# Four array quarters for the scan's products of two head pairs, and a normalised input made by scaling and plain transposes

## The chip, the cores and the metric

The kernel runs on one core of one Trainium2 chip. The metric is the device time of one execution in microseconds (us). Single durations are given in us or ns.

## What is computed

A two-layer block for 1024 latent tokens and a context of 256 tokens, width 1024. Each layer normalises and modulates its input, projects it with one large matrix, feeds four groups with the columns, multiplies each group's output by its own gate path, and projects back. Group A is a gated DeltaNet with 4 heads of width 64, scanned forward and backward over chunks of 64 tokens; the context runs first and hands its states to the latent tokens.

```python
def rmsnorm(x, g):
    return x * rsqrt(mean(x * x, -1) + EPS) * g
...
h = rmsnorm(x, norm_g[l]) * (1.0 + scale) + shift        # latent; the same for the context
p = h @ w_in[l]
...
# one chunk of the scan, per head; tinv, attn, w, u come from the chunk's own keys and gates
def step(s, xs):
    qg_i, kdec_i, u_i, w_i, attn_i, gl_i = xs
    v_new = u_i - w_i @ s
    o_i = qg_i @ s + attn_i @ v_new
    s = s * gl_i + einsum('bhcd,bhce->bhde', kdec_i, v_new)
    return s, o_i
```

## The kernel before

**How the program is ordered.** Every operation is recorded with the tiles it reads and writes (`Program.record`, `add`). Then `schedule` deals the operations to five engines (PE, ACT, DVE, POOL, SP) by estimated costs (`estimate`), by a priority that is the place in the program less a boost (the scans' is 800), and by when pool buffers come free. The result is a fixed order on each engine. All DMAs go out from SP's queue, in its order. All operations are recorded by one helper, so every row of the trace shows line L214; the names of tiles tell the work apart (`sc`, `ax`, `mm` are PSUM tiles; `mm` is the projections').

**The streams.** Threads write the program: for each layer a context stream and a latent stream. `dense` runs the projections one after the other (products of 128x512, `mm<-hh,w`, `mm<-hl,w`); they are what PE does between the instructions of scans, inversions and normalisations.

**The normalised input.** A tile x of 128 tokens by 1024 gets its factor r per token from `h_stat`. `h_diag` writes the diagonal matrix diag(r) on DVE (`dg`); `h_cols` takes it as the moving operand of four fp32 products per half tile, x(128x128)ᵀ·diag(r), which scale and transpose at once, and splits the modulated result in two parts for the projections. There are 20 tiles: 2 of the context and 8 latent ones at the start, and 10 at the layer boundary (`hstage`, whose tiles 0 to 7 also store the new x to DRAM first).

**Heads and halves.** 64 rows of the array hold one half p of the partitions. `st.qk[hh]`, with hh the pair of heads (0 and 1, or 2 and 3), has head 2·hh + p on half p. The state S is [128, 2 (direction d), 2 (hh), 64], with the same halves.

**Before the scan.** `pair_matrices` forms the chunk matrices and stores them to DRAM: three DMAs `zd<-b` per call, 20 calls. `invert` reads them back as single rows, inverts blocks of 32, and `prep` in `scan` puts together the inverse `Ts` and the matrices `ATs` for four chunks at a time. `gdn` makes decays (`ex`), norms (`norms`) and gates.

**The scan.** One step handles chunk s forward and chunk n−1−s backward. For each of the 8 combinations of d, hh and p there is one product of each kind, 64x64 by 64x64 in fp32, two instructions each:

- kS (bank A, part 0), then x = kS · gate + nk on DVE
- out of the step before (AT · v1), then `out_add`
- T·x (bank A, part 1), then v2 on DVE and v1 on ACT
- qS (bank Bk, part 0), then at = qS · gate on DVE
- Sp = kstᵀ · v2, then S = gs + Sp on DVE

All of them read rows of half p and write columns of half p, as in

```python
self.mm(A[half[p], 0, d, hh, :], st.qk[hh][half[p], 1, tok(d)], S[half[p], d, hh, :])
```

PSUM banks: `psx` rotates through four scan banks and `ax`; a scan holds banks 0 to 3 for A, Sp and two Bk.

## Time and profile before

| | |
|---|---|
| median of 3 runs | 1384.72 us (1384.66 to 1385.25) |
| profiled execution | 1382.8 us |
| its span | 1381.1 us |
| mean granted TensorE clock | 0.969 of 2.4 GHz |
| PE / DVE / ACT busy | 1299.9 / 986.2 / 539.9 us |

How to read it: the profiled execution is one run with its own time; the span is what the trace covers of it, 1.7 us less. The busy time of PE counts products; weight loads (PEld) run beside them. Matmuls are pipelined and overlap, so a group's mean duration is more than its distance from one start to the next; prices per instruction are therefore read from starts in a timeline. The first 165 us hold the modulation vectors, the first normalisations and the first projections; layer 0 goes on to about 680 us; at the boundary (to about 797 us) layer 0's output projection makes the new x; then comes layer 1, with its pair matrices and context scan before and its latent scan from about 1108 to 1206 us, and the output projection in the last 80 us.

### The profile page before, as it was taken

How to read it: one execution, taken by the hardware profiler on the slowest of the kernel's cores; microseconds unless marked ns; L12 is line 12 of the kernel's file. 1: busy time of each engine (PE TensorE's matmuls, PEld its weight loads, DVE VectorE, ACT ScalarE, POOL GpSimd, SP SyncE). 2: the span in 40 equal slices, each digit the busy share in tenths (PEclk: the TensorE clock that was granted, in tenths of full speed). 3: DMA queues.
4: the chain of work that ended last, by engine and by line, in shares of the span. 5: the costliest groups of instructions: out<-in, count | busy, mean ns of one | idle time of the engine just before them, and what ended most of it. 6: DMA issues, size and time to landing. Idle time of an engine off the chain costs nothing.

```text
span 1381.1 us, 27009 instructions
## 1 busy us (share of the span) xinstructions
PE 1299.9 (94%) x10992; PEld 1047.1 (76%) x10992; DVE 986.2 (71%) x2102; ACT 539.9 (39%) x903; POOL 11.9 (1%) x76
## 2 busy tenths in 40 slices
PE   6887899999999999999999999998999888999997
PEld 4886778987778666678887788987777776788886
DVE  3888959999869755753466659899788866753554
ACT  4877433254644221321244355343475121231221
POOL 1000000000000000000000000000000000000000
PEclk9988899999999999999999999999899989999999
DMA  9748232322485566561333341523237533122831
GB/s 306 213 109 242 58 74 70 86 47 61 111 203 145 151 198 190 185 184 54 109 115 111 100 113 51 128 54 88 66 99 178 121 80 100 49 76 96 269 82 56
DMA packets 308465, 166.74 MB, mean 121 GB/s; under 512 B 148254, under 2 KB 292982, under 8 KB 308342
## 3 DMA queue, kind: packets, MB, share of 16 engines
q1 hardware_dynamic: 308342, 165.03, 43.3%
q8 instruction: 86, 1.41, 0.4%
q14 instruction: 37, 0.30, 0.1%
HBM read 124.32 MB, written 35.42 MB: 116 GB/s over the span
## 4 chain that ended last, share of the span: by engine, by line
PE 60%; DVE 15%; DMA 14%; ACT 3%; issue 3%; SPq 3%; ACTq 0%; DVEq 0%
PE mm L214 45%; PE sc L214 11%; DVE u L214 8%; DMA x<-u 6%; PE ax L214 5%; DVE b L214 3%; SPq L214 3%; DMA r<-in_w_in 3%; DVE w L214 2%; DMA u<-in_w_out 2%; ACT u L214 1%; DMA whh<-in_w_ada 1%; DMA whl<-in_w_ada 1%; DMA u<-in_x 1%; DMA b<-zb 1%
## 5 line engine op out<-in xcount | busy, mean ns | idle before, releaser
L214 PE MATMUL mm<-hh,w 128*128 128x512 f32 x1664 | 541.4, 401 | 1.7 <-ACT w L214 1.2
L214 PEld LDWEIGHTS mm<-hh,w 128*128 128x128 f32 x1664 | 311.8, 190 | 82.0 <-issue 16.5
L214 PE MATMUL mm<-hl,w 128*128 128x512 f32 x832 | 334.3, 402 | 0.0
L214 PE MATMUL mm<-u,w 128*128 128x512 f32 (+1 forms) x1320 | 261.5, 356 | 1.6 <-ACT g L214 1.1
L214 PEld LDWEIGHTS mm<-u,w 128*128 128x128 f32 x1320 | 220.0, 193 | 35.3 <-ACT g L214 1.7
L214 DVE SCALAR_TENSOR_TENSOR u<-u,pv,u 128x1024 f32<-128x1024 f32 (+1 forms) x172 | 201.9, 1182 | 1.0
L214 PEld LDWEIGHTS mm<-hl,w 128*128 128x128 f32 x832 | 157.9, 190 | 40.7 <-issue 9.3
L214 ACT CAST w<-r 128x1024 fp32r<-128x1024 f32 x88 | 92.5, 1051 | 214.4 <-PE mm L214 159.2
L214 ACT ACT_TABLE_LOAD x94 | 120.6, 1283 | 17.7 <-DMA zd<-b 5.9
L214 DVE TENSOR_TENSOR w<-r,w 128x1024 fp32r<-128x1024 f32 x88 | 107.2, 1218 | 27.3 <-ACT w L214 26.8
L214 DVE TENSOR_TENSOR u<-u,b 128x256 f32<-128x256 f32 (+25 forms) x246 | 89.3, 378 | 26.5 <-DMA u<-in_x 16.3
L214 PE MATMUL mm<-u,u 128*128 128x256 f32 (+1 forms) x384 | 56.5, 299 | 9.8 <-ACT u L214 4.2
L214 DVE TENSOR_TENSOR b<-u 128x108 f32<-128x108 f32 (+21 forms) x180 | 56.5, 323 | 7.0 <-DMA u<-zd 3.8
L214 PEld LDWEIGHTS mm<-u,u 128*128 128x128 f32 x384 | 51.2, 200 | 12.8 <-DVE u L214 5.0
L214 ACT ACTIVATE b<-u 128x512 f32<-128x512 f32 (+1 forms) x71 | 42.5, 609 | 40.4 <-DVE u L214 29.4
L214 PEld LDWEIGHTS sc<-v,u 64*64 64x64 f32 x1184 | 40.3, 138 | 16.0 <-DVE v L214 9.9
L214 PEld LDWEIGHTS sc<-s,u 64*64 64x64 f32 x1168 | 40.6, 141 | 15.1 <-DVE s L214 4.5
L214 PE MATMUL sc<-s,u 64*64 64x64 f32 x1168 | 47.3, 230 | 2.3 <-DVE u L214 1.7
L214 PE MATMUL sc<-v,u 64*64 64x64 f32 x1184 | 46.6, 226 | 2.5 <-DVE v L214 1.3
L214 PE MATMUL mm<-u,hh 128*128 128x272 f32 x256 | 48.5, 289 | 0.0
L214 ACT ACTIVATE b<-sc,mod,modG 128x128 f32<-128x128 f32 x76 | 30.9, 459 | 44.5 <-PE sc L214 26.9
L214 PE MATMUL sc<-dg,u 128*128 128x128 f32 x248 | 38.2, 311 | 8.7 <-issue 4.7
(271 smaller groups left out, 1451.8 us busy)
## 6 DMA issues: line engine op xcount, KB each, us to landing
r<-in_w_in SPq DMA_DIRECT2D x90, 512.0 KB
u<-in_w_ada SPq DMA_DIRECT2D x16, 1024.0 KB
u<-in_x SPq DMA_DIRECT2D x16, 512.0 KB
r<-ylat SPq DMA_DIRECT2D x16, 512.0 KB
zd<-b SPq DMA_DIRECT2D x60, 128.0 KB
ylat<-g SPq DMA_DIRECT2D x24, 256.0 KB
u<-in_w_out SPq DMA_DIRECT2D x12, 512.0 KB
at<-b SPq DMA_DIRECT2D x36, 128.0 KB
```

The costliest lines, as they stand in the source:

```text
L214: op.alts[e] = ((lambda fn=fn, ar=ar, k=k: fn(*ar, **k)), cost, table)
```

## The change

**Quarters.** For heads 2 and 3 (hh = 1) one side of q, k, the state's partner tensors and the chunk matrices is kept on the other half: the row half of a product is p, its column half p ^ hh. `S`, `v2` and `kst` stay as they were, so kS and qS go from half p to half p ^ hh, T·x goes back, out goes over again, and Sp stays on its half. For that, the gates (`gd`), `nkv` (`shuffle`), the `zd` stores and the rows of `w_out` are written flipped for hh = 1, and the decays and norms get small products that carry a half across (`Rm` split in columns, `pf`): seven more per stream, four streams. Each hh has its own PSUM bank (`scan_pair`, [128, 2, 512]).

**Order in a step.** qS and out are written right behind kS, in one pair of banks Bk with Sp; at comes ahead of the step's gs and v2.

**Stores.** Each of the three `zd` stores of a call becomes three: 60 become 180.

**Input.** `h_turn` scales half a tile by r (`affine`, on ACT or DVE as the planner deals it) and turns it with four plain transposes. `h_diag` goes.

**Planner.** A transpose is estimated at 0.12 us, was 0.218; the least for small products is 0.116, was 0.15; quads are divided by 4; dependences in PSUM go by bank, were by tile.

```diff
+    def scan_pair(self, k):
+        return self.nc.own(self.sc.tile([P, 2, 512], F32, tag=f"sc{k}", name=self.nm("sc")), f"sc{k}", 1)
...
-    def h_diag(self, r):
-        dg = self.small("dg", [P, P])
-        self.nc.vector.tensor_scalar(dg, self.ident, r, None, ALU.mult)
-        return dg
+    def h_turn(self, x, r, half):
+        xr = self.blk([P, 4, P])
+        self.affine(xr, x[:, half * 512:(half + 1) * 512].rearrange("p (k c) -> p k c", c=P), r)
+        ps = self.psx([P, 4, P])
+        for k in range(4):
+            self.tr(ps[:, k, :], xr[:, k, :], self.ident)
+        self.free("b")
+        return ps
...
-            ps = self.psx([P, 4, P])
-            for k in range(4):
-                kk = half * 4 + k
-                self.mm(ps[:, k, :], x[:, kk * P:(kk + 1) * P], dg)
+            ps = self.h_turn(x, r, half)
...
-            nc.sync.dma_start(zd[d, 2 * s0:2 * s0 + 4].rearrange("c p i -> p c i"), t)
+            to = zd[d, 2 * s0:2 * s0 + 4].rearrange("(c h) p i -> h p c i", h=2)
+            t = t.rearrange("p (c h) i -> p h c i", h=2)
+            nc.sync.dma_start(to[0], t[:, 0])
+            for p in range(2):
+                nc.sync.dma_start(to[1, (1 - p) * TC:(2 - p) * TC], t[p * TC:(p + 1) * TC, 1])
...
-            A = self.scan_bank(0, [P, 2, 2, 2, HD])
+            A = pair(0, 2)
+            Bk = pair(1, 3) if need_o or not last else None
+            into = lambda bank, r, kind: quads((bank[half[p ^ hh], r, d, hh, :], st.qk[hh][half[p], kind, tok(d)],
+                                                S[half[p], d, hh, :]) for d, hh, p in each)
...
-                for d, hh, p in each:
-                    self.mm(A[half[p], 0, d, hh, :], st.qk[hh][half[p], 1, tok(d)], S[half[p], d, hh, :])
+                into(A, 0, 1)
...
+            if need_o and not first:
+                into(Bk, 0, 0)
             if pend:
-                out(*pend)
-                out_add(*pend)
+                out(Bk, *pend)
+                out_add(Bk, *pend)
+            at = None
+            if need_o and not first:
+                at = self.small("at", sh)
+                nc.vector.tensor_tensor(at, Bk[:, 0], sg(1), ALU.mult)
...
-            for d, hh, p in each:
-                self.mm(A[half[p], 1, d, hh, :], Ts[j % 2][half[p], d, 2 * (G - 1 - i if d else i) + hh, :], x[half[p], d, hh, :])
+            quads((A[half[p], 1, d, hh, :], Ts[j % 2][half[p ^ hh], d, 2 * (G - 1 - i if d else i) + hh, :],
+                   x[half[p ^ hh], d, hh, :]) for d, hh, p in each)
...
-                if not first:
-                    for d, hh, p in each:
-                        self.mm(Bk[half[p], 0, d, hh, :], st.qk[hh][half[p], 0, tok(d)], S[half[p], d, hh, :])
```

What the planner makes of it is seen on three queues.

PE in layer 1's latent scan, one step; `x` is x, `v_` of before's `sc_1592` is v1 for out, `s_94` the state, `u_` the chunk matrices, keys and queries; before:

```order
L214 MATMUL sc_1585<-s_94,u_1237 64x64 x2
L214 MATMUL mm_1509<-hl_978,w_1469 128x512
L214 MATMUL mm_1509<-hh_977,w_1469 128x512 x2
L214 MATMUL sc_1581<-x_1582,u_1414 64x64 x8
L214 MATMUL mm_1509<-hl_978,w_1469 128x512
L214 MATMUL mm_1509<-hh_977,w_1469 128x512 x2
L214 MATMUL sc_1592<-v_1487_1586,u_1239 64x64 x8
L214 MATMUL sc_1585<-v_1488_1587,u_1414 64x64 x8
L214 MATMUL mm_1509<-hl_978,w_1469 128x512
L214 MATMUL sc_1593<-s_94,u_1236 64x64 x2
```

and with the change:

```order
L215 MATMUL sc_1525<-s_94,u_1201 64x64 x2
L215 MATMUL sc_1525<-v_1423_1522,u_1370 64x64 x8
L215 MATMUL mm_1478<-hh_940,w_1450 128x512
L215 MATMUL mm_1478<-hl_941,w_1450 128x512
L215 MATMUL mm_1478<-hh_940,w_1450 128x512 x2
L215 MATMUL mm_1478<-hl_941,w_1450 128x512
L215 MATMUL mm_1478<-hh_940,w_1450 128x512
L215 MATMUL sc_1524<-x_1526,u_1370 64x64 x8
L215 MATMUL mm_1478<-hh_940,w_1450 128x512
L215 MATMUL mm_1478<-hl_941,w_1450 128x512
L215 MATMUL mm_1478<-hh_940,w_1450 128x512 x2
L215 MATMUL sc_1525<-v_1431_1530,u_1203 64x64 x8
```

qS and out moved from behind T·x to kS, and more projection products stand between the groups: from the first to the last T·x of this scan the order before has 71 of them (narrower ones counted by their width), and with the change 136.

PE at the layer boundary, where a tile's normalised input is turned (`u_956` is x, `b_1015` the scaled half); before:

```order
L214 MATMUL mm_1050<-u_934,w_1025 128x512
L214 MATMUL sc_1052<-dg_1051,u_956 128x128 x4
L214 MATMUL mm_1050<-u_934,w_1025 128x512 x2
L214 MATMUL mm_1050<-u_936,w_1025 128x512
L214 MATMUL sc_1054<-dg_1051,u_956 128x128 x4
L214 MATMUL mm_1050<-u_936,w_1025 128x512 x2
```

and with the change:

```order
L215 MATMUL mm_1014<-u_896,w_989 128x512
L215 MATMUL sc_1016<-ident_100,b_1015 128x128 x4
L215 MATMUL mm_1014<-u_896,w_989 128x512 x2
L215 MATMUL mm_1014<-u_899,w_989 128x512
L215 MATMUL sc_1016<-ident_100,b_1018 128x128 x4
L215 MATMUL mm_1014<-u_899,w_989 128x512 x2
```

The turns stand in the same places; the operand is the scaled half in place of x and the diagonal.

SP while the pair matrices of layer 0's latent stream are stored (`at` are the matrices for out, `u_562` the inversion's rows); before:

```order
L214 DMA zd_563<-b_585 128x4x64 x2
L214 DMA at_561<-b_586 128x256 x2
L214 DMA zd_563<-b_590 128x4x64
L214 DMA u_562<-zd_563 32x32x32
L214 DMA u_632<-u_505 32x16x32 x3
L214 DMA u_644<-at_561 128x512
L214 DMA zd_593<-b_594 128x4x64 x2
```

and with the change:

```order
L215 DMA zd_550<-b_556 128x2x64
L215 DMA zd_550<-b_556 64x2x64
L215 DMA at_548<-b_557 128x256 x2
L215 DMA zd_550<-b_556 64x2x64
L215 DMA zd_550<-b_556 128x2x64
L215 DMA zd_550<-b_556 64x2x64 x2
L215 DMA u_624<-at_548 128x512
L215 DMA zd_550<-b_560 128x2x64
L215 DMA zd_550<-b_560 64x2x64 x2
```

Three stores stand where one stood, and the inversion's first read (`u_549<-zd_550` there) has moved some 40 entries further down, behind stores of the second group of chunks (`zd_576`).

## Rows read from the trace of the kernel before

**Rows 1.** Page: engines' busy us, share, instructions; then the chain by engine.

```profile
PE 1299.9 (94%) x10992; PEld 1047.1 (76%) x10992; DVE 986.2 (71%) x2102; ACT 539.9 (39%) x903; POOL 11.9 (1%) x76
PE 60%; DVE 15%; DMA 14%; ACT 3%; issue 3%; SPq 3%; ACTq 0%; DVEq 0%
```

**Rows 2.** Stages: us, busy PE, PEld, DVE, ACT, POOL (instructions), PEclk, DMA share, GB/s.

```profile
0.00:165.00 165.00, 130.52 (x1007) 115.93 (x1008) 125.88 (x388) 108.44 (x212) 5.31 (x46) 0.91 0.66 191
165.00:680.00 515.00, 505.07 (x4682) 385.95 (x4681) 363.47 (x687) 175.33 (x261) 2.67 (x12) 0.99 0.46 125
...
797.00:1050.00 253.00, 248.22 (x1773) 203.73 (x1772) 219.92 (x389) 123.03 (x178) 2.42 (x8) 0.97 0.37 90
...
1108.00:1206.00 98.00, 88.59 (x1756) 69.25 (x1757) 65.17 (x153) 23.48 (x50) 0.00 (x0) 0.93 0.28 75
```

**Rows 3.** Timeline of PE, 540 to 560 us: start, us, form, instructions.

```profile
541.77 1.15 PE L214 MATMUL sc<-s,u 64*64 64x64 f32 x32
542.85 1.58 PE L214 MATMUL ax<-u,u 128*64 128x128 f32 x16
...
548.79 0.75 PE L214 MATMUL ax<-b,b 32*32 32x32 f32 x64
549.47 0.50 PE L214 MATMUL mm<-hl,w 128*128 128x512 f32 x1
...
558.26 0.68 PE L214 MATMUL sc<-x,u 64*64 64x64 f32 x16
558.87 0.59 PE L214 MATMUL ax<-b,sel 128*2 128x256 f32 x2
```

**Rows 4.** One-column run (timeline), and stages inside a run on shared rows.

```profile
422.40 2.75 PE L214 MATMUL sc<-ones,b 64*64 64x1 f32 x88
...
274.24:274.50 0.26, 0.25 (x4) 0.26 (x5) 0.00 (x0) 1.00 0.00 0
274.50:274.68 0.18, 0.18 (x10) 0.18 (x9) 0.00 (x0) 1.00 0.00 0
```

**Rows 5.** Timelines of PE where tiles are turned: boundary, start, and transposes.

```profile
802.46 3.73 PE L214 MATMUL sc<-dg,u 128*128 128x128 f32 x32
805.94 0.48 PE L214 MATMUL mm<-hl,w 128*128 128x512 f32 x1
...
128.80 3.47 PE L214 MATMUL sc<-dg,u 128*128 128x128 f32 x16 [2.27 <-issue]
...
584.38 1.70 PE L214 MATMUL sc<-ident,u 128*128 128x128 f32 x12
586.01 0.59 PE L214 MATMUL ax<-b,sel 128*2 128x256 f32 x2
```

**Rows 6.** Groups by form: operation, busy us, mean ns of one, idle before.

```profile
L214 DVE TENSOR_SCALAR aux<-aux,rs 128x512 f32<-128x512 f32 x1 | 0.5, 486 | 0.0
L214 ACT ACTIVATE aux<-aux,rs 128x512 f32<-128x512 f32 x1 | 0.7, 722 | 1.0 <-DVE rs L214 1.0
L214 DVE TENSOR_SCALAR dg<-ident,rs 128x128 f32<-128x128 f32 x20 | 5.6, 281 | 0.4
```

**Rows 7.** Chain of 690 to 830 us, and a timeline row of PE there.

```profile
by line: DMA x<-u 59.0%; PE mm L214 16.9%; DMA r<-in_w_in 5.4%; DVE w L214 3.5%; issue 3.1%; DMA u<-in_ctx 2.6%; DVE u L214 2.0%; PE sc L214 1.9%; SPq L214 1.8%; ACT u L214 1.6%; ACT w L214 0.7%; DVE b L214 0.5%; DVE rt L214 0.4%; DVE ss L2
689.90 7.25 PE mm L214 x32
708.09 13.46 DMA x<-u
...
749.85 1.16 PE L214 MATMUL ax<-dg,u 128*128 128x128 f32 x8 [1.16 <-DVE dg L214]
```

**Rows 8.** SP's stores to zd (ns least/median/most), and chain of 380 to 475 us.

```profile
L214 SPq DMA_DIRECT2D zd<-b x60: 360/470/1896, 92.5 to 1069.6; - x60
by line: SPq L214 18.4%; PE sc L214 15.4%; PE mm L214 13.3%; DVE u L214 11.6%; DVE b L214 10.0%; DMA zb<-u 5.6%; DMA at<-b 5.4%; issue 4.5%; PE ax L214 3.5%; DMA gd<-g 2.8%; DMA b<-zb 2.7%; ACT L214 1.4%; DVE w L214 1.2%; DMA b<-in_b_ada 1.
```

**Rows 9.** DVE's operation of the form of at, least/median/most ns.

```profile
L214 DVE TENSOR_TENSOR x<-sc,sg x38: 405/424/426, 196.0 to 1202.2; 128x256 f32<-128x256 f32 x38
```

More of the change, by code (lines that the diff above doesn't have):

```diff
@@ L223, in add @@
                         continue
[L224 removed]
+                    reg = self.region(a)
                 else:
@@ L477, in __init__ @@
         self.n = self.xi = self.scanning = 0
+        self.other = None
         self.W = Weave()
@@ L517, in psx @@
     def psx(self, shape):
-        self.xi = (self.xi + 1) % 5
-        if self.scanning or self.xi == 4:
-            return self.nc.own(self.ax.tile(shape, F32, tag="ax", name=self.nm("ax")), "ax", 1)
-        return self.scan_bank(self.xi, shape)
-    def scan_bank(self, k, shape):
-        return self.nc.own(self.sc.tile(shape, F32, tag=f"sc{k}", name=self.nm("sc")), f"sc{k}", 1)
+        if self.scanning:
+            self.other = None
+        t, self.other = self.other, None
+        if t is None:
+            self.xi = (self.xi + 1) % 3
+            if self.scanning or self.xi == 2:
+                return self.nc.own(self.ax.tile(shape, F32, tag="ax", name=self.nm("ax")), "ax", 1)
+            pair = self.scan_pair(self.xi)
+            t, self.other = pair[:, 0], pair[:, 1]
+        n = 1
+        for x in shape[1:]:
+            n *= x
+        t = t[0:shape[0], 0:n]
+        if len(shape) == 3:
+            t = t.rearrange("p (a b) -> p a b", b=shape[2])
+        elif len(shape) == 4:
+            t = t.rearrange("p (a b c) -> p a b c", b=shape[2], c=shape[3])
+        return t
+    def scan_pair(self, k):
+        return self.nc.own(self.sc.tile([P, 2, 512], F32, tag=f"sc{k}", name=self.nm("sc")), f"sc{k}", 1)
     def mm(self, out, lhsT, rhs, start=True, stop=True):
@@ L1343, in gdn @@
         pe = self.psx([P, 6, m])
+        half = [slice(p * TC, (p + 1) * TC) for p in range(2)]
         for d in range(2):
-            self.mm(pe[:, d], self.Rm[d], g[:, d])
+            self.mm(pairs(pe)[:, d, :, 0], self.Rm[d], pairs(g)[:, d, :, 0])
+            for p in range(2):
+                self.mm(pairs(pe)[half[p], d, :, 1], self.Rm[d][:, half[1 - p]], pairs(g)[:, d, :, 1])
             self.mm(pe[:, 2 + d], self.Lm[d], g[:, d])
@@ L1366, in gdn @@
         st.nk = V("nk", 1)[:, 0]
-        nc.vector.tensor_tensor(st.nk, nq[:, 1], rn[:, 1], ALU.mult)
+        nc.vector.tensor_tensor(t[:, 1], nq[:, 1], rn[:, 1], ALU.mult)
+        pf = self.psx([P, 1, m])
+        self.mm(pairs(pf)[:, 0, :, 0], self.ident, pairs(t)[:, 1, :, 0])
+        for p in range(2):
+            self.mm(pairs(pf)[half[p], 0, :, 1], self.ident[:, half[1 - p]], pairs(t)[:, 1, :, 1])
+        nc.vector.tensor_copy(st.nk, pf[:, 0])
         wd = S("wd", [P, 2, 32])[:, :, :m]
@@ L1419, in norms @@
         nc, n = self.nc, st.n
-        pq = self.psx([P, 2 * n])
-        for b0, nb in st.blocks:
-            for hh in range(2):
+        for hh in range(2):
+            pq = self.psx([P, n])
+            for b0, nb in st.blocks:
                 yield self.room("b")
@@ L1584, in scan, with quads, out, out_add @@
         pend = None
-        def out(s, i, bank, v1, at):
-            AT = ATs[s // G % 2]
-            for d in range(2):
-                for hh in range(2):
-                    e = 2 * (G - 1 - i if d else i) + hh
-                    for p in range(2):
-                        self.mm(bank[half[p], 1, d, hh, :], AT[half[p], d, e], v1[half[p], d, hh, :])
-        def out_add(s, i, bank, v1, at):
+        pair = lambda k, r: self.scan_pair(k)[:, :, 0:r * P].rearrange("p h (r d e) -> p r d h e", r=r, d=2)
+        def quads(calls):
+            nc.quads = True
+            for c in calls:
+                self.mm(*c)
+            nc.quads = False
+        def out(bank, s, i, v1, at):
+            AT = ATs[s // G % 2]
+            quads((bank[half[p ^ hh], 1, d, hh, :], AT[half[p], d, 2 * (G - 1 - i if d else i) + hh], v1[half[p], d, hh, :])
+                  for d, hh, p in each)
+        def out_add(bank, s, i, v1, at):
             oc = st.o[:, two_of(s, n - 1 - s)].rearrange("p d (h e) -> p d h e", h=2)
@@ L1603, in out_add @@
                 self.two(oc, oc, ot, ALU.add)
+        each = [(d, hh, p) for d in range(2) for hh in range(2) for p in range(2)]
         yield from prep(0)
@@ L1650, in scan @@
                 nc.scalar.copy(v1, A[:, 1])
-                if not first:
-                    at = self.small("at", sh)
-                    nc.vector.tensor_tensor(at, Bk[:, 0], sg(1), ALU.mult)
-                pend = (s, i, Bk, v1, at)
+                pend = (s, i, v1, at)
             yield STEP[1]
@@ L1672, in scan @@
         if need_o:
-            out(*pend)
-            out_add(*pend)
+            Bk = pair(1, 3)
+            out(Bk, *pend)
+            out_add(Bk, *pend)
         self.scanning -= 1
```

56 lines of the change are left out of this document (26 added, 30 removed).

## The prediction

> **What bounds the kernel now.** I read the engine line of the page first, then a table of busy time by stage, then the chain of waits, and last the timelines of the instructions that the change touches. The engine line gives TensorE (PE) 94% of the span, VectorE (DVE) 71%, ScalarE (ACT) 39%; the chain of work that ended last lies on PE for 60% and on DVE and DMA for 15% and 14% [rows 1]. The stages tell these apart [rows 2]. From 165 to 680 us (layer 0: pair matrices, both scans, most projections) PE is busy 505 of 515 us, from 797 to 1050 us (layer 1 up to its latent scan) 248 of 253: there a microsecond taken off PE is a microsecond off the kernel, as long as other products stand ready. In layer 1's latent scan (1108 to 1206 us) it is less full, 88.6 of 98 us, so 9.4 us are waits. In the first 165 us no engine is full (PE 131, DVE 126, ACT 108), and from 680 to 797 us the chain lies on a row of stores: 59% of its time is the store of x, 13.5 us for one, one after the other [rows 7].
>
> **The scan's products.** Four kinds of product per step (kS, qS, T·x, out) now use all four 64x64 quarters of the array, where before only the two on the diagonal worked. By the loop, the context scan of layer 0 has 112 of them (T·x and out in 4 steps of 8, kS and qS in 3), that of layer 1 has 56 (no outputs), and each latent scan 16 x 4 x 8 = 512: together 1192. An fp32 product is two instructions, so 2384. Their present price: a run of 32 starts at 541.77 and the next work at 542.85 us, 1.08 us; a run of 16 takes 558.26 to 558.87, 0.61 [rows 3]. The difference, 0.47 us for 16 more, is 29.4 ns each, with two quarters running side by side, so that one quarter spends 58.8 ns on each. Four at once would be 14.7 ns. The unknown is whether two row halves can feed the same 64 columns at once; no row shows that. Bounds: 14.7 ns if they can; 29.4 if they can't, since two would still pair; above that only if the new sequence also broke the old pairing, for which I see no cause, because neighbours in it still differ in rows and in columns. Two rows speak for the low end. The 32x32 products, four at once, go 64 from 548.79 to 549.47, 0.68 us, 10.6 ns each, so neither issue nor weight loads stop at 14.7 [rows 3]. And where 128-row products of the two column halves share their rows, 10 start in 0.18 us inside a run whose first 4 took 0.26 [rows 4]: sharing rows doesn't keep them apart there. A run with one moving column still takes 2.75 us for 88 = 31 ns [rows 4], so the price is that of a quarter's whole turn, weights and all, and another quarter hides it as well as a second one does now. I take 14.7: 2384 x 14.7 ns = **−35.0 us**, of which 30.1 in the latent scans.
>
> Here the Trainium skill speaks against the change. "TensorE: Matmul & The Clock Gate", Part 3, The mechanism, says that weight loads overlap running products only where the row groups differ; by that, heads 2 and 3 would queue behind heads 0 and 1 on the same rows and the sum would lack its 35 us. The shared rows of [rows 4] disagree with it. "TensorEngine Tiling (Array Packing)", Gotcha 1, says that row tiles can't use one PSUM bank at once; the change gives each head its own bank, and no run of before shows the matter.
>
> Is the freed time used? The new order puts 65 more projection products of 128x512 inside layer 1's latent scan. At 0.227 us each (32 in 7.25 [rows 7]) that is 14.8 us of later work drawn forward, about the 15.1 that this scan frees. The filler exists, so I count the whole.
>
> **Small products added.** Seven more per stream for the crosswise decays and norms, 28 in all, 56 instructions. No row shows their form: as the one-column run they cost 31 ns [rows 4], 1.7 us together; as the full-array diagonal product 0.109 us (below), 6.1 us. They lie between in size, so the middle: **+3.9 us**.
>
> **The normalised input.** Twenty tiles, each in two halves, lose 20 diagonal matrices on DVE (0.281 us each) and 160 fp32 products (320 instructions); they get 40 scalings of 128x512 (ACT 0.722 or DVE 0.486 us, [rows 6]) and 160 transposes. Warm, 32 instructions of the old form take 802.46 to 805.94 = 3.48 us, 0.109 each, 0.87 us per half; at the start of the kernel 16 take 3.47, 0.217 each. Transposes of fp32 128x128 take 584.38 to 586.01 for 12, 0.136 each, 0.54 per half [rows 5]. By place:
> Tiles 0 to 7 of layer 1 (680 to 797 us): each waits for SP's sequence of loads and stores, the store alone 13.5 us a tile, PE too (1.16 us before one run [rows 7]). The change leaves that sequence as it is, and a shorter turn only makes PE wait longer: **0**. If the cover went, 16 halves x 0.33 = 5.3 us would come off.
> Tiles 8 and 9: 4 halves x (0.87 − 0.54) on a full PE: **−1.3 us**.
> First 165 us, 10 tiles: PE loses 160 instructions, 17.4 us warm or 34.7 cold, middle 26, and gets 80 transposes, 10.9; at PE's 79% there, the gain ends at 15.1 x 0.79 = 11.9. If instead DVE and ACT set the pace, 20 scalings at the mean of 0.6 us less 10 diagonals are +9.3. No engine is full, so the middle: **−1.3 us**.
>
> **Stores of the pair matrices.** Each call now issues 9 instead of 3 DMAs to zd, 60 become 180. SP issues one in 0.470 us [rows 8], so 120 are 56.4 us of SP; 48 of them, 22.6 us, go in front of each latent scan. Queued behind them on SP are the at stores, the inversion's reads of zd, and weight loads. Between 380 and 475 us SP's queue is 18.4% of the chain [rows 8], over the whole span 3% [rows 1]. By these shares 56.4 us would cost 10.4 or 1.7. A later scan mostly swaps places with projections, of which both layers have many left behind the scan, so I stay near the low end: **+3 us**, bounds 0 and 22.6 per layer.
>
> **The order in a step.** DVE now takes at (qS times a gate) ahead of v2; the same form costs 0.424 us [rows 9]. Over the 33 steps that have both (15 in each latent scan, 3 in layer 0's context scan) that is 14.0 us added to a chain on DVE that leads to T·x's successor and to S. Projections cover it where they stand ready; in layer 1's scan 9.4 of 98 us were uncovered, 10%, so **+1.4 us**, bounds 0 and 14.0. The move of qS forward costs PE nothing: the same products, grouped.
>
> **Sum.** −35.0 + 3.9 − 1.3 − 1.3 + 3 + 1.4 = −29.3 us. The profiled execution took 1382.8 us, which becomes 1353.5; the median of the runs shown is 1.9 higher, 1384.7, so **1355.4 us**. With each term but the first at its better end: −35 + 1.7 − 1.3 − 11.9 = −46.5, 1338.2. With small products, first stage, stores and step order at 6.1, +9.3, +10.4 and +1.4 the time is 1375.6.
>
> **Rivals.**
> 1. The chain of a step becomes the bound. The scan frees PE time, but a step still goes kS, x, T·x, v2, S with DVE between each, and what DVE gets in addition comes before v2. The 9.4 us of waits in layer 1's scan speak for it, the full PE of layer 0 and the 65 products drawn forward against. If half of the latent scans' 30.1 us is waited away: 1355.4 + 15 = 1370.4.
> 2. The quarters don't run together: products that share a column half wait for each other. For it: no row of before has two row halves on one column half. Against: the 32x32 rows and the shared rows. Then the 35 us are missing: 1355.4 + 35 = 1390.4, slower than before by 6. It decides the sign once a product costs over about 27 ns per instruction, since the other terms sum to +5.7.
> 3. The store queue. If layer 0's and layer 1's scans both start 22.6 us later and the projections behind them don't fill PE meanwhile, 45.2 takes the place of the 3: 1355.4 + 42.2 = 1397.6, slower. It changes sign once more than 32 us of the slip go uncovered. For it: 18.4% of the chain between 380 and 475 us; in the new order the inversion's first read of layer 0's latent zd stands behind the second group's stores. Against: the same stretch has PE full, and the projections behind.
> 4. A least distance between two starts of 64x64 products, somewhere between the 14.7 ns that four quarters would need and today's 29.4. For it: the run with one moving column keeps 31 ns although it moves almost nothing [rows 4]. Against: the 32x32 run at 10.6 ns [rows 3]. Halfway, at 22 ns, 2384 x 7.3 = 17.4 of the 35 us are missing: 1372.8. "TensorE: Matmul & The Clock Gate", Part 1, of the Trainium skill gives such a floor, about 25 ns however narrow the product; by it 24.5 us would be missing, 1379.9. The 32x32 run disagrees with it.
>
> **Chances.** Forecast (quarters at 14.7 ns, 1338 to 1366) 0.62; rival 1 with its milder and harder kinds (1366 to 1380) 0.22; rival 2 0.08; rival 3 0.05; rival 4 0.03. About 0.2%, 2.8 us, is what a measurement of this kernel can tell from no change. Forecast, rival 1 and rival 4 are faster by more: 0.87. Rival 2 with a better first stage can end within 0.2%: 0.03 of its 0.08; the other 0.05 and rival 3 are slower: 0.10. The range runs from 1338 to 1378: it leaves out rivals 2 and 3 and the far ends of 1 and 4, some 0.17.
>
> **What the profile after would show.** Right, if a group of 32 quads in the latent scans starts in about 0.5 us where before it took 1.08; if PE in layer 1's latent scan shows about 65 more 128x512 products and the stage behind it is some 15 us shorter; if the turns of a half take 0.54 us; if the store of a tile still takes its 13.5 us and sets the pace there. Wrong, if the quads still start 29 ns apart (rival 2) or somewhat less (rival 4); if PE waits longer in the scan than the 9.4 us, before S or v2 (rival 1); if SP's zd stores come late and the reads of zd, the inversion and the scan behind them, with PE idle (rival 3); or if the first stage grows because ACT or DVE is behind with scalings.

## The result, and the profile after

| | before | after |
|---|---|---|
| median | 1384.69 us (1384.63 to 1385.25, 4 runs) | 1417.68 us (1414.79 to 1429.54, 4 runs) |
| ratio | | 1.0248, interval 1.0213 to 1.0283 |
| profiled execution, its span | 1382.8, 1381.1 us | 1418.2, 1416.1 us |
| granted clock, mean | 0.969 | 0.943 |

The change makes the kernel 33 us slower. The forecast was 29 us faster, with a range that ended at 1378. The page's engine line and the chain by engine, to be read against [rows 1]:

```profile
PE 1277.3 (90%) x10888; PEld 1003.2 (71%) x10888; DVE 986.6 (70%) x2112; ACT 544.9 (38%) x917; POOL 11.9 (1%) x76
PE 52%; DVE 20%; DMA 12%; SPq 7%; ACT 5%; issue 4%; DVEq 0%; ACTq 0%; POOL 0%; POOLq 0%
```

PE works 23 us less, as intended, in a span that is 35 us longer. Its share of the chain falls from 60% to 52%; SP's queue grows from 3% to 7%, DVE from 15% to 20%. The granted clock is lower too: a mean of 0.943 over 1416 us leaves 81 us short of full speed, where 0.969 over 1381 us leaves 43. The difference, 38 us, is an estimate from these means of what the clock added, and rather too large, since the clock is also low while PE waits. The stages of after (us, busy PE, PEld, DVE, ACT, POOL with instructions, granted clock, DMA share, GB/s), cut where the same work stands in [rows 2]:

```profile
0.00:175.00 175.00, 124.28 (x943) 105.28 (x944) 129.81 (x395) 115.65 (x216) 5.09 (x42) 0.88 0.64 180
175.00:706.00 531.00, 503.28 (x4694) 375.94 (x4694) 360.04 (x689) 167.60 (x257) 2.86 (x16) 0.95 0.45 121
706.00:822.00 116.00, 108.64 (x498) 88.08 (x497) 76.78 (x187) 52.16 (x115) 1.16 (x5) 0.99 0.35 110
822.00:1085.00 263.00, 251.88 (x1780) 203.57 (x1780) 219.09 (x387) 126.27 (x183) 1.31 (x6) 0.98 0.35 82
1085.00:1164.00 79.00, 52.96 (x460) 42.50 (x460) 52.87 (x153) 17.71 (x24) 1.47 (x7) 0.79 0.49 110
1164.00:1256.00 92.00, 86.30 (x1849) 62.85 (x1839) 67.04 (x152) 26.42 (x53) 0.00 (x0) 0.94 0.33 87
1256.00:1416.00 160.00, 149.95 (x692) 125.02 (x690) 80.92 (x154) 39.09 (x70) 0.00 (x0) 0.98 0.41 125
```

The first stage takes 175 us for 165; layer 0 takes 531 for 515; the boundary 116 for 117; layer 1 up to its latent scan 342 us (822 to 1164) for 311 (797 to 1108). Then the change does what it was forecast to do: the scan 92 for 98, with more projections in it, and the last stage 160 for 175. So 56 us are lost up to layer 1's latent scan, and 21 gained from there on. The worst stretch, 1085 to 1164 us, has PE busy 53 of 79 us. Its longest wait stands right in front of the scan: PE's products of the inversion wait 12.2 us for DVE, which inverts what SP read back late. The reads of zd in before and in after (ns least/median/most, first and last start), and PE's row:

```profile
L214 SPq DMA_DIRECT2D u<-zd x24: 567/618/1416, 114.4 to 1080.6; - x24
L215 SPq DMA_DIRECT2D u<-zd x24: 562/624/2412, 126.3 to 1134.8; - x24
1161.56 1.18 PE L215 MATMUL ax<-b,b 32*32 32x32 f32 x64 [12.20 <-DVE b L215]
```

The last read is 54 us later than in before, and the scan's first T·x 57 (1164.9 for 1108.1); 26 us of both were lost by the end of layer 0 (706 us for 680).

The scan's products first. A timeline of PE in after's layer 1 scan (start, us, form, instructions):

```profile
1213.92 0.69 PE L215 MATMUL sc<-s,u 64*64 64x64 f32 x32
1214.44 0.41 PE L215 MATMUL sc<-v,u 64*64 64x64 f32 x16
1214.78 0.74 PE L215 MATMUL mm<-hh,w 128*128 128x512 f32 x2
```

32 instructions of kS and qS take 0.52 us where [rows 3] had 1.08, and 16 of out take 0.34. That is 16 ns each for the 32, near the 14.7 of the forecast: four quarters do run at once, also with two row halves on one column half. The single starts in the trace show the same: four products start within 0.02 us, and the next four 0.058 us after them. In before two start together, and the next two also come 0.058 us later. So a turn of the array takes the same 58 ns with two quarters as with four.

Now layer 0's pair matrices. The stores of after, the chain of 385 to 520 us by line (cut by the view), what ACT and DVE waited for from 385 to 450 us (us in total, times, longest), PE's timeline there, and the stage of 420 to 500 us:

```profile
L215 SPq DMA_DIRECT2D zd<-b x180: 366/588/2339, 102.9 to 1122.8; - x180
by line: SPq L215 25.9%; DVE b L215 10.9%; DVE u L215 10.0%; PE mm L215 8.4%; issue 8.0%; PE sc L215 8.0%; PE ax L215 7.5%; DMA zb<-u 4.2%; DMA zd<-b 3.6%; DMA gd<-g 3.6%; DMA u<-zd 2.9%; DVE w L215 2.7%; DMA b<-zb 1.9%; ACT w L215 0.8%; DV
ACT b L215 <- DMA zd<-b: 20.6, 5, 7.6
DVE b L215 <- DMA zd<-b: 6.5, 3, 3.3
DVE b L215 <- ACT b L215: 4.4, 4, 2.4
420.18 0.61 PE L215 MATMUL mm<-hh,w 128*128 128x512 f32 x2
426.82 0.71 PE L215 MATMUL sc<-s,u 64*64 64x64 f32 x16 [6.02 <-DVE b L215]
427.46 0.79 PE L215 MATMUL mm<-hl,w 128*128 128x512 f32 x1
...
436.91 1.06 PE L215 MATMUL mm<-hh,w 128*128 128x512 f32 x2
437.76 0.63 PE L215 MATMUL mm<-hl,w 128*128 128x512 f32 x1
...
420.00:500.00 80.00, 66.07 (x533) 49.41 (x535) 49.66 (x157) 17.16 (x27) 0.31 (x2) 0.74 0.60 147
```

This is the loss in one place. SP issues 180 stores at a median of 588 ns, 106 us, where [rows 8] had 60 at 470, 28 us. The buffers of the chunk matrices come free only when their stores have left. ACT, which writes the next ones, waits 20.6 us for that; DVE waits 6.5 us for stores itself and 4.4 for ACT; and PE waits 6.02 us for DVE. PE's queue is fixed: projections stand behind the product that waits (kS, `sc<-s,u`), can't pass it, and start at once when it is through, with no wait of their own (427.46). After the wait PE runs at half its speed for a while, 1.2 GHz in place of 2.4 (two 128x512 products take 0.85 us, 436.91 to 437.76, where [rows 7] has 0.227 for one), and the stretch of 420 to 500 us has a mean granted clock of 0.74.

### The profile page after: what moved, and what is told of

It is laid out like the page before. It is cut to its first block, busy times and chain, and to the rows that moved or that the text cites. A ratio compares the mean times of both kernels' runs of the same rounds, so it can differ in the third digit from the quotient of the medians.

```text
span 1416.1 us, 27022 instructions
## 1 busy us (share of the span) xinstructions
PE 1277.3 (90%) x10888; PEld 1003.2 (71%) x10888; DVE 986.6 (70%) x2112; ACT 544.9 (38%) x917; POOL 11.9 (1%) x76
## 4 chain that ended last, share of the span: by engine, by line
PE 52%; DVE 20%; DMA 12%; SPq 7%; ACT 5%; issue 4%; DVEq 0%; ACTq 0%; POOL 0%; POOLq 0%
PE mm L215 37%; DVE u L215 10%; PE sc L215 10%; SPq L215 7%; PE ax L215 5%; DVE b L215 5%; DMA x<-u 3%; DMA r<-in_w_in 3%; DVE w L215 2%; ACT b L215 1%; DMA u<-zd 1%; ACT L215 1%; DMA zd<-b 1%; ACT u L215 1%; DMA u<-in_x 1%
## 5 line engine op out<-in xcount | busy, mean ns | idle before, releaser
L215 PE MATMUL mm<-hh,w 128*128 128x512 f32 x1664 | 553.9, 407 | 6.8 <-ACT g L215 4.2
L215 PEld LDWEIGHTS mm<-hh,w 128*128 128x128 f32 x1664 | 316.1, 192 | 92.0 <-issue 20.8
L215 PE MATMUL mm<-hl,w 128*128 128x512 f32 x832 | 338.8, 407 | 1.5 <-issue 1.5
L215 DVE TENSOR_TENSOR u<-u,b 128x256 f32<-128x256 f32 (+26 forms) x246 | 90.1, 387 | 28.1 <-DMA u<-in_x 17.9
L215 DVE TENSOR_TENSOR b<-u 128x198 f32<-128x198 f32 (+24 forms) x180 | 56.9, 331 | 8.5 <-DMA u<-zd 6.9
L215 PE MATMUL sc<-ident,b 128*128 128x128 f32 (+1 forms) x139 | 27.5, 322 | 25.2 <-ACT b L215 10.2
L215 PEld LDWEIGHTS sc<-v,u 64*64 64x64 f32 x1184 | 34.4, 140 | 19.6 <-DVE v L215 11.2
L215 ACT COPY v<-sc 128x256 f32<-128x256 f32 x36 | 13.4, 372 | 78.6 <-PE sc L215 69.4
L215 ACT ACTIVATE b<-sc,mod,modG 128x128 f32<-128x128 f32 x86 | 35.0, 456 | 19.4 <-PE sc L215 11.0
L215 PEld LDWEIGHTS sc<-ident,b 128*128 128x128 f32 (+1 forms) x139 | 18.9, 163 | 32.6 <-ACT b L215 13.5
```

Of the source, the lines that this page charges most:

```text
L215: op.alts[e] = ((lambda fn=fn, ar=ar, k=k: fn(*ar, **k)), cost, table)
```

## Experiments: the two parts, and the stores

Four kernels separate the parts. The theory, S: the 120 added stores on SP cost the time. Rivals: H, the turn by scaling; O, the new order of a step. Of each kernel the ratio to the kernel before on the same chip is given; 1% is 13.8 us.

**The turn alone**, in the kernel before:

```diff
-                self.mm(ps[:, k, :], x[:, kk * P:(kk + 1) * P], dg)
+            ps = self.h_turn(x, r, half)
```

> The kernel before with the input turned by scaling and plain transposes, and nothing else (its planner's costs kept). Theory S (the 120 more stores on SP delay the inversions and with them the scans): the turn is not what costs, 1378 to 1388 us. Rival H (the scalings on ACT and DVE hold up the first stage and what follows): 1395 or more, with the first 165 us longer by 10 or more. Rival O (the new order and the chain of a scan step): 1378 to 1390.

Measured: 1389.3 us, 1.0016 (0.9984 to 1.0049). No difference that can be told.

**The quarters alone**, the changed kernel with the diagonal turn:

```diff
-            self.tr(ps[:, k, :], xr[:, k, :], self.ident)
...
+            kk = half * 4 + k
+            self.mm(ps[:, k, :], x[:, kk * P:(kk + 1) * P], dg)
```

> The changed kernel with the input turned by the diagonal products as before. Theory S: all of the loss stays, 1405 to 1420 us. Rival H: the loss goes and the scans' gain shows, 1355 to 1375. Rival O: 1405 to 1420.

Measured: 1401.8 us, 1.0099 (1.0066 to 1.0132). Theory S expected all of the loss to stay; 13.7 us stay and some 20 go. So in the changed kernel the turn costs, though it didn't alone.

**Three stores**, both parts, with the flip of heads 2 and 3 in DRAM left out:

```diff
-            to = zd[d, 2 * s0:2 * s0 + 4].rearrange("(c h) p i -> h p c i", h=2)
-            t = t.rearrange("p (c h) i -> p h c i", h=2)
-            nc.sync.dma_start(to[0], t[:, 0])
-            for p in range(2):
-                nc.sync.dma_start(to[1, (1 - p) * TC:(2 - p) * TC], t[p * TC:(p + 1) * TC, 1])
+            nc.sync.dma_start(zd[d, 2 * s0:2 * s0 + 4].rearrange("c p i -> p c i"), t)
```

> The changed kernel with three zd stores a call as before in place of nine; the halves of heads 2 and 3 are not flipped in DRAM, so that these heads' outputs are not the reference's, while all work but the six stores is there. Theory S: the slip at the pair matrices goes and the quarters' gain shows, 1355 to 1375 us. Rival H: 1400 to 1415. Rival O: 1395 to 1415, with the same waits of PE inside the scans.

Measured: 1380.9 us, 0.9949 (0.9919 to 0.9978). The stores are worth 1.0248 − 0.9949 = 3.0%, 41 us, in the changed kernel. But the result isn't the 1355 to 1375 of theory S: some 25 us of the forecast gain are missing for other reasons.

**Nine stores**, in the kernel before:

```diff
-            nc.sync.dma_start(zd[d, 2 * s0:2 * s0 + 4].rearrange("c p i -> p c i"), t)
+            to = zd[d, 2 * s0:2 * s0 + 4].rearrange("(c h) p i -> h p c i", h=2)
+            t = t.rearrange("p (c h) i -> p h c i", h=2)
+            nc.sync.dma_start(to[0], t[:, 0])
+            for p in range(2):
+                nc.sync.dma_start(to[1, p * TC:(p + 1) * TC], t[p * TC:(p + 1) * TC, 1])
```

> The kernel before with each zd store cut in three as in the changed kernel, same data to the same places, 120 DMAs more on SP and nothing else. Theory S: 1415 to 1440 us, with SP's queue without gaps where the pair matrices are stored. Rivals H and O: within 10 us of before, 1384 to 1395.

Measured: 1434.9 us, 1.0319 (1.0272 to 1.0366). The same data to the same places costs 44 us when SP issues it in 180 pieces. Its stores, and its waits of PE from 1050 to 1170 us:

```profile
L214 SPq DMA_DIRECT2D zd<-b x180: 366/594/1771, 93.3 to 1123.1; - x180
PE ax L214 <- issue: 14.0, 1, 14.0
PE sc L214 <- DVE b L214: 8.7, 3, 8.0
```

180 at 594 ns are 107 us of SP, 79 more than before, and over half of that lands on the kernel's time. No quarter and no turn is in it, so the stores alone turn a gain into a loss. What the longest wait (14.0 us) waited for the profile doesn't show.

## Experiments: what is left without the stores

The runs of this section that have quarters or two quarters, and three stores, leave the flip of heads 2 and 3 in DRAM out, as the run above.

**Quarters, diagonal turn, three stores:** the second and the third diff above together.

> The changed kernel with the diagonal turn and three zd stores a call (the halves of heads 2 and 3 not flipped in DRAM, so their outputs are not the reference's; all other work is there). Theory S now says that the stores cost some 41 us in the changed kernel and the turn some 10 in its first stage: 1360 to 1372 us, ratio 0.980 to 0.990. Rival O (the new order of a step and its interleaving eats the quarters' gain): 1376 to 1388, ratio 0.992 to 1.000.

Measured: 1366.3 us, 0.9878 (0.9842 to 0.9915), within what theory S expected. Against nine stores (1.0099) that is 2.2%, 31 us. Its chain between 380 and 475 us lies on PE, and SP's queue, 25.9% of the chain in after's stretch, has 2.2%:

```profile
by line: PE mm L215 47.8%; PE sc L215 15.2%; DVE b L215 8.0%; DMA zd<-b 6.8%; PE ax L215 6.1%; issue 4.9%; DVE u L215 4.8%; DMA u<-u 2.5%; SPq L215 2.2%; ACT u L215 0.8%; ACT b L215 0.6%; DVE nq L215 0.2%; DVEq L215 0.2%; ACT L215 0.1%; ACT
```

**Two quarters**, the same kernel with heads 2 and 3 on the diagonal (the line of out; kS, qS and T·x likewise):

```diff
-            quads((bank[half[p ^ hh], 1, d, hh, :], ...
+            quads((bank[half[p], 1, d, hh, :], ...
```

> The run with three stores, but the four kinds of product of heads 2 and 3 read and write the same half as those of heads 0 and 1, so that only two quarters work (these heads' outputs are not the reference's; the count of products and the order are the same). If the quarters bring what the prediction said and the freed time is used: 28 to 36 us more than with quarters. If the chain of a step sets the pace (rival 1): under 15 more.

Measured: 1396.2 us, 1.0104 (1.0063 to 1.0146). Between these two runs the quarters are worth 1.0104 − 0.9878 = 2.3%, 31 us, with some 8 us either way by the two intervals: the size of the forecast's first term (35.0, or 30.1 in the latent scans). A timeline of PE in its layer 1 scan:

```profile
1147.04 1.15 PE L215 MATMUL sc<-s,u 64*64 64x64 f32 x32
1148.02 0.63 PE L215 MATMUL sc<-v,u 64*64 64x64 f32 x16
1148.59 0.45 PE L215 MATMUL ax<-b,b 32*32 32x32 f32 x30
```

0.98 us for 32 and 0.57 for 16, against 0.52 and 0.34. But with two quarters this kernel is 1.0%, 14 us, above before, though it has before's stores and turn.

**The old order of a step**, quarters and three stores:

```diff
-            if need_o and not first:
-                into(Bk, 0, 0)
             if pend:
...
+            if need_o and not first:
+                into(Bk, 0, 0)
             if not last:
                 v2 = self.small("v2", sh)
```

> The run with three stores, but qS behind T*x and at behind v2 and v1 as before the change. The prediction's term for the step order says 1.4 us less than with the new order, bounds 0 and 14; rival O says 10 us or more less.

Measured: 1375.1 us, 0.9938 (0.9912 to 0.9964). The old order is 0.6%, 8 us, slower, though the intervals just touch; so with four quarters the new one seems to help, and the forecast had it cost 1.4.

**The planner's new estimates alone**, in the kernel before:

```diff
-                return 0.218
+                return 0.12
...
-                return max(0.15, 0.05 + n * 4 / 2400.0) / self.side_by_side(k, m)
+                return max(0.116, 0.01 + n * 4 / 2400.0) / self.side_by_side(k, m)
```

> The kernel before with the planner's new estimates for transposes and small products, and nothing else. If the planner's new order is what costs the 14 us by which the run with two quarters is above before: 1392 to 1400. If the estimates change little: 1380 to 1388.

Measured: 1383.1 us, 0.9992 (0.9973 to 1.0011): nothing.

**The old estimates**, with quarters and three stores (the reverse diff, quads still divided by 4):

> The run with quarters, diagonal turn and three unflipped stores (heads 2 and 3 not the reference's), planned with the estimates of before (a transpose 0.218, small products from 0.15; quads still a quarter of one). If the new estimates cost: 1352 to 1362 us; if they help: 1370 to 1380; if they change little, as the run with the new ones, 1366, within 4.

Measured: 1375.4 us, 0.9949 (0.9927 to 0.9971). Worse by 0.7% than with the new ones, which here are nearer to the trace: a scan product (two instructions) takes 32 ns, the new estimate is 29, the old one 39.

**Bank pairs alone**, in the kernel before:

```diff
-            A = self.scan_bank(0, [P, 2, 2, 2, HD])
+            AS = self.scan_pair(0)
+            A = five(AS[:, 0])
...
-                Sp = self.scan_bank(1, sh)
+                Sp = five(AS[:, 1])[:, 0]
```

> The kernel before with the change's PSUM handling alone: tiles of two banks, handed out as halves and freed together, and dependences by bank. If the run with two quarters is 14 us above before for this reason: 1392 to 1400 us. If not: 1380 to 1388.

Measured: 1384.5 us, 1.0007 (0.9990 to 1.0025): nothing.

**The small products alone**, in the kernel before, everything on its own half:

```diff
-            self.mm(pe[:, d], self.Rm[d], g[:, d])
+            self.mm(pairs(pe)[:, d, :, 0], self.Rm[d], pairs(g)[:, d, :, 0])
+            for p in range(2):
+                self.mm(pairs(pe)[half[p], d, :, 1], self.Rm[d][:, half[p]], pairs(g)[:, d, :, 1])
```

> The kernel before with the change's extra small products alone (decays and norm factors cut by half and head pair, norms in one tile per head pair), all on the same half as before. The prediction's term is 3.9 us, bounds 1.7 and 6.1: 1386 to 1391 us. If the 14 us of the run with two quarters come from here: 1394 or more.

Measured: 1391.8 us, 1.0051 (1.0026 to 1.0077): 7 us, between 3.6 and 10.7. The forecast's 3.9 lies in the interval, near its lower end. The norms in one tile per head pair, which this kernel also has, had no price in the forecast.

**Two quarters in the old order**, the diffs of the run with two quarters and of the one with the old order together:

> The run with two quarters and three stores, but with qS and at where they stood before the change (heads 2 and 3 not the reference's). What is left between it and the kernel before are the small products (7 us by their own run) and what the planner makes of it. If the new step order costs when two quarters work, as the prediction had it: about 1390 us. If the order isn't it: 1394 to 1402.

Measured: 1403.3 us, 1.0120 (1.0094 to 1.0146), not below the run with two quarters. So the order isn't it, and neither are estimates or bank pairs on their own. Half of the 14 us may be the small products (3.6 to 10.7); the rest is open. One rival wasn't tested: in both runs with two quarters the planner still divided a scan product by four, 29 ns, where it takes 61 (0.98 us for 32 instructions). What a plan for two quarters would take off the 14 us, and so off the 31 us between two quarters and four, isn't known; the run with the old estimates shows that wrong prices (for these products and for transposes) can go with 10 us.

## Experiments: keeping the quarters without the stores

**The flip on DVE.** The operation that forms the chunk matrices is cut in three and writes heads 2 and 3 to the other half; three stores, diagonal turn:

```diff
-        nc.vector.tensor_tensor(gx, both(1), dm, ALU.mult)
...
+        hs = [(slice(0, P), slice(0, P), 0), (half[1], half[0], 1), (half[0], half[1], 1)]
+        for o, i, h in hs:
+            nc.vector.tensor_tensor(gx[o, :, h::2], both(1)[i, :, h::2], dm[i, :, h::2], ALU.mult)
```

> Quarters with the diagonal turn, three zd stores a call, and the flip made by the DVE operation that forms the chunk matrices: it is cut in three (heads 0 and 1 on all partitions, and heads 2 and 3 of each half written to the other half), some 0.35 us of DVE more per call, 20 calls, 7 us of DVE. Theory S: within 5 us of the run with three unflipped stores, 1360 to 1377 us, faster than both kernels. Rival: DVE, which is in the chain of the pair matrices, gives back 7 us or more: 1375 to 1390.

Measured: 1383.8 us, 0.9998 (0.9978 to 1.0017); the rival was right. Groups by form (busy us, mean ns, idle before), the last one from before:

```profile
L215 DVE TENSOR_TENSOR b<-sc,b 64x256 f32<-64x256 f32 x32 | 13.5, 422 | 2.0 <-PE sc L215 1.6
L215 DVE TENSOR_TENSOR b<-sc,b 128x256 f32<-128x256 f32 x16 | 6.7, 418 | 0.5
L214 DVE TENSOR_TENSOR b<-sc,b 128x512 f32<-128x512 f32 x32 | 20.9, 681 | 0.9 <-PE sc L214 0.6
```

Half the partitions cost as much as all, 422 against 418 ns: three operations of 0.42 us for one of 0.68, 0.58 us more per call, 11.6 in all, on the engine that the pair matrices wait for. The kernel lost 1.2%, 17 us, against the run without a flip; the 5 us beyond the 11.6 aren't traced.

**Other queues.** Nine stores, of which the six for heads 2 and 3 go out from ACT, or from POOL:

```diff
-                nc.sync.dma_start(to[1, (1 - p) * TC:(2 - p) * TC], t[p * TC:(p + 1) * TC, 1])
+                nc.scalar.dma_start(to[1, (1 - p) * TC:(2 - p) * TC], t[p * TC:(p + 1) * TC, 1])
```

(with `nc.gpsimd` in the other; the planner counts an issue as 0.475 us on ACT and 1.0 on POOL).

> Quarters with the diagonal turn and nine stores a call, of which the six that carry heads 2 and 3 go out from ACT's queue in place of SP's (the planner deals them as operations of ACT with the time of an SP issue). Theory S (SP's queue is what the stores fill): most of the 2.2% between nine and three stores comes back, 1366 to 1380 us. Rival: the stores cost by their landing, since the buffers that hold the matrices come free only then, and by ACT's own time: 1385 to 1400.

> The same with the six stores on POOL's queue, which does nothing else there. Theory S: 1366 to 1380 us. Rival (landing, or POOL slower at issuing than SP): 1385 to 1410.

Measured: ACT 1389.8 us, 1.0045 (1.0020 to 1.0071); POOL 1383.7 us, 1.0006 (0.9982 to 1.0030). Neither is in theory S's 1366 to 1380: ACT lies in the rival's range, POOL just under it. The issues on ACT, on POOL, and what SP still issues beside POOL (ns least/median/most):

```profile
L215 ACTq DMA_DIRECT2D zd<-b x120: 581/618/1934, 94.9 to 1095.1; - x120
L215 POOL DMA_DIRECT2D zd<-b x120: 590/590/762, 93.9 to 1084.0; - x120
L215 SPq DMA_DIRECT2D zd<-b x60: 359/453/1862, 93.6 to 1082.7; - x60
```

An issue of the cut stores costs about 0.6 us on any of the three. With SP relieved, about a quarter (ACT) or two fifths (POOL) of the 2.2% comes back. So SP's queue is part of the price. On ACT the waits stay: ACT and DVE wait 46 us in all for zd stores, against 44 with all nine on SP and 14 with three. On POOL, which has next to nothing else to do, they wait only 17 us, though one call's six stores still take POOL 3.5 us; so what keeps that kernel 1.3% above the one with three stores isn't shown.

**Queries off the diagonal.** The last version asks which products have to change halves. If kS and T·x of all heads stay on the diagonal, and qS and out of all heads go to the other half, then kS with qS, and T·x with out, fill four quarters, and only the outputs change halves. No chunk matrix moves: three stores, nkv and the norms of k as before.

```diff
-                into(A, 0, 1)
+                quads(weave(into(A, 0, 1), into(Bk, 0, 0) if need_o else []))
...
-            quads((A[half[p], 1, d, hh, :], Ts[j % 2][half[p ^ hh], ...
+            quads(weave([(A[half[p], 1, d, hh, :], Ts[j % 2][half[p], ...], out(Bk, *pend) if pend else []))
```

> All four quarters without a flip of the chunk matrices: kS and T*x of all heads stay on the diagonal, qS and out of all heads go to the off-diagonal quarters, issued between kS and T*x two by two. Only the outputs change halves, so that the zd stores stay three a call, and nkv and the norms of k stay as before; four small products for the query's decays are added. The turn is the diagonal one. If stores and nothing else stood between the quarters' gain and the clock: 1352 to 1370 us, faster than both kernels. Rival O (order and bank pairs cost 14 us whatever the stores): 1364 to 1372. Rival: T*x, now slowed by out beside it, and out's later end hold up a step: 1375 or more.

Measured: 1364.0 us, 0.9868 (0.9845 to 0.9892), 18 us faster than before and 3.7% faster than the changed kernel. It lies in the ranges of theory S and of rival O alike (1352 to 1370, 1364 to 1372), so it doesn't decide between them; that T·x holds up the step (1375 or more) is out. Its page (engines, chain), its stores and PE in a step:

```profile
PE 1280.7 (94%) x11016; PEld 1019.1 (75%) x11016; DVE 980.2 (72%) x2087; ACT 549.6 (40%) x918; POOL 11.9 (1%) x76
PE 69%; DMA 10%; DVE 10%; SPq 4%; ACT 4%; issue 2%; ACTq 0%; DVEq 0%
L215 SPq DMA_DIRECT2D zd<-b x60: 359/484/1096, 94.5 to 1064.6; - x60
1169.71 0.69 PE L215 MATMUL sc<-s,u 64*64 64x64 f32 x32
1170.34 0.73 PE L215 MATMUL mm<-hh,w 128*128 128x512 f32 x2
...
1171.70 0.27 PE L215 MATMUL sc<-x,u 64*64 64x64 f32 x2
1171.71 0.27 PE L215 MATMUL sc<-v,u 64*64 64x64 f32 x2
...
1172.17 0.22 PE L215 MATMUL sc<-v,u 64*64 64x64 f32 x2
1172.32 0.50 PE L215 MATMUL mm<-hl,w 128*128 128x512 f32 x1
```

PE carries 69% of the chain, more than the 60% of before, and has 19 us less work. T·x and out of 32 instructions share 0.62 us.

**The turn on top of it:**

```diff
-            kk = half * 4 + k
-            self.mm(ps[:, k, :], x[:, kk * P:(kk + 1) * P], dg)
+        self.affine(xr, x[:, half * 512:(half + 1) * 512].rearrange("p (k c) -> p k c", c=P), r)
...
+            self.tr(ps[:, k, :], xr[:, k, :], self.ident)
```

> The kernel with the query's products off the diagonal, with the input turned by scaling and plain transposes. By the pairs of runs so far the turn costs between 2 us (alone) and 14 (with quarters and three stores): 1366 to 1378 us, the loss standing in the first 165 us.

Measured: 1362.7 us, 0.9831 (0.9798 to 0.9863), 0.4% below the run with the diagonal turn, with intervals that overlap: no difference that can be told. The expectation (2 to 14 us slower) was wrong; the forecast's 2.6 us of gain are neither shown nor excluded.

## Why the prediction was wrong

**The step that failed** is the one on the stores: "A later scan mostly swaps places with projections, of which both layers have many left behind the scan, so I stay near the low end: +3 us". It measured 31 us (quarters, nine against three stores), 41 (with the turn too) and 44 (in the kernel before). Two things were wrong in it. The cover was taken for work that is ready; but PE takes its queue in a fixed order, and the projections stand behind the small products that wait. And the wait was looked for only at the scan's start, in the late reads. It does stand there in layer 1 (12.2 us of PE for the inversion), but the stores also hold the buffers of the matrices, so that ACT, DVE and PE stand within the pair matrices too (20.6 us of ACT, 6.02 of PE in layer 0, in one place). The price of an issue, 0.470 us, was too low as well: the 180 take 0.588, so that SP got 78 us more and not 56.4. The bounds of the step, 22.6 us per layer, did cover the 41; rival 3 was the right mechanism, with 1397.6 us, and got a chance of 0.05. Its row for it, the 18.4% of SP in the chain of 380 to 475 us [rows 8], pointed the right way, but as a price it gave 10.4 us, a quarter of the cost: a queue's share of the chain before a change doesn't say what it holds up when it is filled further.

**The quarters** were right: 16 ns for the forecast 14.7, worth some 31 us in these plans; rivals 2 and 4 fall with the timeline of after. The Trainium skill's "TensorE: Matmul & The Clock Gate" would have had weight loads wait where rows are shared (Part 3, The mechanism), and starts at least about 25 ns apart (Part 1); the 32 instructions in 0.52 us disagree with both. The Trainium skill's "TensorEngine Tiling (Array Packing)", Gotcha 1, says that row tiles can't use one PSUM bank at once. The prediction took the change to give each head its own bank, and no run of before to show the matter; both are wrong. The change gives one bank to each pair of heads, so the row halves p = 0 and p = 1 write one bank (other partitions of it), as they do in A of before, where the two start together, 0.007 us apart, and the next two 0.058 us later. Neither kernel shows one waiting for the other. Two row halves that write the same columns have different banks in all these runs; what one bank would do there wasn't tried.

One row was misread. A count in a table by stages holds every instruction that runs in the stretch, not only those that start there, so the "10 start in 0.18 us" of [rows 4] is too many: the run has 16, and the view's three stretches count 26 (4, 10 and 12). By the single starts 7 fall into that stretch. That shared rows don't keep products apart is still what they show.

```profile
274.25 0.92 PE L214 MATMUL sc<-nat,ident 128*64 128x32 f32 x16
```

**The freed time** was used: the last stage of after is 15 us shorter, as forecast. Rival 1 falls too; in layer 1's latent scan PE is idle 5.7 us of 92, fewer than the 9.4.

**Small products**: 7 measured (3.6 to 10.7) for a forecast of 3.9, which that doesn't exclude. **The step order** seems to have had the wrong sign: with four quarters the run with the old order is 8 us slower, with two no difference can be told.

**The turn.** The boundary is right: the eight stores of x run from 706.0 to 804.9 us in after, 98.9 us, and from 680.3 to 779.4 before, 99.1; the stores set the pace there whatever PE does. The turn itself got shorter than forecast: four transposes take 0.36 us (711.14 to 711.50), not 0.54.

```profile
L214 SPq DMA_DIRECT2D x<-u x8: 497/497/589, 680.3 to 779.4; - x8
L215 SPq DMA_DIRECT2D x<-u x8: 497/497/601, 706.0 to 804.9; - x8
711.14 0.60 PE L215 MATMUL sc<-ident,b 128*128 128x128 f32 x4
711.50 10.46 PE L215 MATMUL mm<-u,w 128*128 128x512 f32 x45
```

In the first stage it was mis-sized, and not by a constant. It cost nothing that can be told alone, 20 us in the changed kernel (1.0248 against 1.0099), 10 with three stores (0.9949 against 0.9878), and nothing that can be told beside the queries off the diagonal. In after, PE waits in the first 175 us for ACT, once in front of a scaled half:

```profile
PE sc L215 <- ACT b L215: 11.8, 8, 3.4
149.54 1.33 PE L215 MATMUL sc<-ident,b 128*128 128x128 f32 x5 [3.42 <-ACT b L215]
```

But this wait doesn't tell the kernels apart: in the first 165 us it is 13.2 us in the run with the quarters alone, which has no scalings, and 11.0 with the turn alone, which lost no time. What all four pairs share is the clock: from 100 to 165 us the granted clock is 0.71 with the turn alone for 0.84 before, 0.74 in after for 0.92 with the diagonal turn, 0.71 for 0.79 with three stores, and 0.76 for 0.87 beside the queries off the diagonal. The stretch in before, with the turn alone, with the quarters alone and in after (columns as in [rows 2]):

```profile
100.00:165.00 65.00, 49.93 (x360) 46.35 (x359) 57.45 (x169) 43.13 (x88) 1.55 (x10) 0.84 0.56 153
100.00:165.00 65.00, 43.87 (x292) 39.70 (x292) 56.02 (x161) 45.56 (x90) 0.39 (x5) 0.71 0.57 151
100.00:165.00 65.00, 49.31 (x377) 45.55 (x378) 53.28 (x156) 42.66 (x93) 1.35 (x6) 0.92 0.55 145
100.00:165.00 65.00, 38.06 (x267) 33.54 (x267) 53.10 (x151) 44.24 (x88) 1.34 (x6) 0.74 0.58 153
```

PE does less there and at a lower clock. The forecast's worse end for this place (+9.3, where ACT and DVE set the pace) fits the 10 us by which the first stage of after is longer, but no run shows that the scalings are the reason. The planner deals the whole program anew for every kernel, and this stage has no engine that is full; why the time is lost in two of the pairs and not in the other two stays open.

**The sum of the parts.** From before to two quarters +14, to four −31, with nine stores +31, with the turn +20: +34. These are steps of one path from before to after, so they must add up to what was measured (34 by the ratio, 33 by the medians), and that they do confirms none of them. On another path the sizes differ: the turn is 20 us after the stores and 10 ahead of them.

## What to carry to other kernels

Price what a layout change does to the transfers before what it does to the arithmetic: here each cut of a store is another 0.6 us on an issuing queue, and the buffer behind it is held until the last piece has left. On engines with a fixed order, work that stands ready behind a waiting instruction covers nothing; look in the queue for what stands in front. And before moving data to where idle parts of the array are, ask which products can go there with only their results changing place.

## What the runs showed of the hardware

Four 64x64 quarters take fp32 products at 16 ns an instruction (32 in 0.52 us), with two products on the same rows and two on the same columns; those that share rows or columns write different banks, those that share neither write the same one. A DVE operation on 64 partitions that writes the other half takes what one on 128 takes (422 and 418 ns). A store of 64 partitions costs about 0.6 us to issue on ACT or POOL (medians of 618 and 590 ns), and on SP the 180 pieces have a median of 588, above that of the 60 whole stores (470). The pieces of 128 partitions aren't dearer: where SP issues them alone, the median is 453.
